# Turning forgetting-attention weights by DMA in 16-bit halves, with the next head's logits ahead of a head's value product

## The chip, the cores and the metric

The kernel runs on one core of a Trainium2 chip. The metric is the device time of one execution, in microseconds (us): the median of several runs. The engines of a core have queues of their own and meet at semaphores: TensorE (PE in the profile, with its weight loads as PEld), VectorE (DVE), ScalarE (ACT), GpSimd (POOL) and SyncE (SP), which here issues nearly all DMA transfers.

## The reference

Two layers act on a sequence of 512 positions of width 1024. Each layer is a SwiGLU half-step, a mixing step, and a second SwiGLU half-step. The change concerns the mixing step, and in it the forgetting attention:

```python
proj = u @ w_in[l]
q_sb, k_sb, v_sb, q_fx, k_fx, v_fx, f_logit, q_mem = split(proj)   # heads: 8 x 64 | 8 x 64 | 4 x 128
o_sb = stick_breaking(q_sb, k_sb, v_sb)
o_fx = forgetting(q_fx, k_fx, v_fx, log_sigmoid(f_logit + b_forget[l]))
o_mem = memory(q_mem, *split(mem_n @ w_mem_kv[l]))
g_sb, g_fx, g_mem = split(sigmoid(u @ w_gate[l] + b_gate[l]))
merged = g_sb * (o_sb @ w_br_sb[l]) + g_fx * (o_fx @ w_br_fox[l]) + g_mem * (o_mem @ w_br_mem[l])
h = h + rmsnorm(merged @ w_out[l])

def forgetting(q, k, v, log_f):           # per head, in four blocks of 128 query positions
    c = cumsum(log_f)
    z = q @ k.T / 8 + c[query] - c[key]
    p = softmax(where(key <= query, z, -inf))
    return p @ v
```

The weights p come out with queries on the partitions. For the value product p @ v the keys have to be on the partitions, so the lower triangle of p, ten blocks of 128 x 128, is transposed.

## The kernel before

**Precision.** Products run in the PE's fp32r format. A value is split into a high part (a cast on ACT) and a low part (a subtraction on DVE) by `split`, lines 182 and 183 of the profile, and a product is the sum of three matmuls (`mm3`, L212 to L214). In the value product of a head, only the weights are split (two matmuls for each of four key blocks).

**What runs beside what.** The mixing step of a layer goes through its heads one after the other: 4 memory heads, 8 stick-breaking heads (tiles with s in their names: `zs`, `ts`, `ns`, `pws`, `pts`, `pvs`), then 8 forgetting heads (tiles with f: `zf`, `pf`, `ptf`, `pvf`). Between a head's steps, PE works on the projections and gates of the same layer (`pq`, `pk`, `pv`, `pg`), of which a list of jobs is kept. A head is a generator that yields either work that it put on PE, `("pe", us)`, or a time that it expects to wait for other engines, `("wait", us)`; `Queue.weave` fills each wait with jobs from the list, as far as a limit for that head allows. Where the list up to the limit is used up, the head goes on at once. The waits are the constants `W_SB0..2` (stick-breaking) and `W_FX0`, `W_FX1` (forgetting). PE's order is so written out; instructions on the other engines which `keep_in_program_order` doesn't hold are put in order by a list scheduler when the program is built. The gates' own evaluation (`ga`: L204 to L208 on ACT and DVE) and the preparation of the branch weights (`wh_wb`, `wl_wb`) also run in this stage. After it come the branch product `pb` (forgetting branch), and the output product (`pwo`).

**A forgetting head** (`fox_head`). Logits go to four banks of PSUM `z`: the causal mask (L1262), q times k (L1269), and the decay (L1270, whose operand `qk` is prepared by `fox_pre` one head ahead). For each query block DVE takes the maximum (L1272), ACT the exponential with its sum (L1274), and DVE the reciprocal and the scaling (L1275, L1276). After a planned wait of 6.5 us `transposed` puts ten transposes on PE (L1185) into the same four banks, and splits the blocks out of PSUM into `ptf`, by four casts on ACT and four subtractions on DVE. After a second wait, of 4.7 us, `attend` multiplies by the values (eight matmuls, L1171, into `pvf`); the sum of the two halves (L1174, L1175) is split into `o`, the operand of the branch product. The heads go in the order of pairs 2, 3, 0, 1, so that the last head of layer 0 is `f0_1_1`. Each head is woven on its own, with a limit of its own.

**A stick-breaking head** turns its weights by another way already. The float32 weights are seen as pairs of 16-bit words. ACT writes the low words and the high words into separate planes (`turn_out`, L1152, tile `ns`), SP issues a DMA transpose of both planes (`turn_over`, L1161, back into `ts`), ACT joins the words again into a float32 tile `pws` (L1237), and the joined tile is split from SBUF in two pieces, 640 and 896 columns wide. This goes by three groups of query blocks: (3,), (2,) and (1, 0), of 1024, 768 and 768 words.

## Time and profile before

| | |
|---|---|
| Time, median of 3 runs | 2339.55 us (2337.33 to 2340.01) |
| Profiled execution: time, span | 2342.67 us, 2340.9 us |
| PE busy | 2322.9 us (99%) |
| DVE busy | 1764.2 us (75%) |
| ACT busy | 1509.8 us (64%) |
| Granted TensorE clock | 0.999 |
| Forgetting heads of layer 0 | about 629 to 766 us of the span |
| Transposes on PE (L1185) | 160, 10 for each of 16 heads |

The profile's rows name the line of the kernel, the engine, the operation and the tiles (out<-in). A timeline row gives the start, the length, and in brackets how long the engine had been idle before and what released it. A row of waits sums the idle time of an engine before a group of instructions by its releaser. Matmuls overlap in the pipeline, so the distance from one start to the next is their cost, not their listed length.

### The profile page before, as it was taken

What the parts mean: (1) busy time and instruction counts of PE and PEld (TensorE: products, weight loads), DVE (VectorE), ACT (ScalarE), POOL (GpSimd) and SP (SyncE); (2) the same over time, 40 slices, a digit from 0 to 9 for tenths busy, and PEclk for the clock granted to TensorE, in tenths of its full rate; (3) what the DMA queues carried; (4) which work ended last, traced back from release to release, by engine and by line L of the source; (5) the groups of instructions that cost most, each with busy time, mean ns of one, the idle gap of its engine ahead of it and who ended that gap; (6) DMA issues with size and microseconds to landing.
All of it is one profiled execution on the core that took longest, in us unless ns stands there. A gap on an engine that the chain in (4) does not pass through costs nothing.

```text
span 2340.9 us, 30650 instructions
## 1 busy us (share of the span) xinstructions
PE 2322.9 (99%) x11463; PEld 1960.2 (84%) x11463; DVE 1764.2 (75%) x2253; ACT 1509.8 (64%) x2216; POOL 81.2 (3%) x182
## 2 busy tenths in 40 slices
PE   9999999999999999999999999999999999999998
PEld 7888888888888888888898888888888888888887
DVE  8877877566777688878798788765677767887785
ACT  6677465577756556775656774655787674667744
POOL 0000000000111000000000000000001100000000
PEclk9999999999999999999999999999999999999999
DMA  6667454344423555674646665544444236466744
GB/s 207 190 176 221 146 189 141 93 115 114 122 73 105 187 186 164 185 199 152 226 144 186 196 185 179 185 114 95 119 105 116 81 118 200 160 195 176 220 138 144
DMA packets 340344, 365.44 MB, mean 156 GB/s; under 512 B 120778, under 2 KB 231650, under 8 KB 340196
## 3 DMA queue, kind: packets, MB, share of 16 engines
q1 hardware_dynamic: 340100, 363.46, 52.0%
q8 instruction: 90, 1.47, 0.3%
q14 instruction: 58, 0.48, 0.1%
q0 software_dynamic: 96, 0.03, 0.0%
HBM read 319.39 MB, written 16.78 MB: 144 GB/s over the span
## 4 chain that ended last, share of the span: by engine, by line
PE 85%; DMA 5%; ACT 4%; DVE 3%; issue 2%; DVEq 0%; SPq 0%; ACTq 0%
PE pg L213 4%; PE pg L212 4%; PE pg L214 4%; PE pda L213 3%; PE pda L212 3%; PE pda L214 3%; PE pdc L213 3%; PE pdc L212 3%; PE pdc L214 3%; PE pb L213 1%; PE pb L212 1%; PE pb L214 1%; PE pq L213 1%; PE pq L212 1%; PE pq L214 1%
## 5 line engine op out<-in xcount | busy, mean ns | idle before, releaser
L212 PE MATMUL pg<-us_a,wh_wg 128*128 128x512 f32 x384 | 150.4, 392 | 0.0
L213 PE MATMUL pg<-us_a,wh_wg 128*128 128x512 f32 x384 | 149.7, 390 | 0.0
L214 PE MATMUL pg<-us_a,wl_wg 128*128 128x512 f32 x384 | 149.6, 390 | 0.0
L183 DVE TENSOR_TENSOR wl_da<-raw_da,wh_da 128x1024 fp32r<-128x1024 f32 x50 | 60.8, 1223 | 44.6 <-ACT wh_da L182 44.4
L183 DVE TENSOR_TENSOR wl_dc<-raw_dc,wh_dc 128x1024 fp32r<-128x1024 f32 x50 | 61.0, 1223 | 44.1 <-ACT wh_dc L182 44.1
L213 PE MATMUL pdc<-wl_dc,ahc 128*128 128x512 f32 x224 | 87.7, 392 | 0.0
L213 PE MATMUL pda<-wl_da,aha 128*128 128x512 f32 x224 | 87.6, 391 | 0.0
L214 PE MATMUL pdc<-wh_dc,alc 128*128 128x512 f32 x224 | 87.2, 389 | 0.0
L214 PE MATMUL pda<-wh_da,ala 128*128 128x512 f32 x224 | 87.2, 389 | 0.0
L212 PE MATMUL pdc<-wh_dc,ahc 128*128 128x512 f32 x224 | 86.6, 390 | 0.5 <-ACT pdc L895 0.5
L212 PE MATMUL pda<-wh_da,aha 128*128 128x512 f32 x224 | 86.5, 389 | 0.0
L186 DVE SCALAR_TENSOR_TENSOR wl_wg<-raw_wg,wh_wg 128x1024 fp32r<-128x1024 f32 x48 | 58.7, 1223 | 35.8 <-ACT wh_wg L185 35.6
L214 PEld LDWEIGHTS pg<-us_a,wl_wg 128*128 128x128 f32 x384 | 72.1, 188 | 15.1
L212 PEld LDWEIGHTS pg<-us_a,wh_wg 128*128 128x128 f32 x384 | 72.1, 188 | 14.2
L213 PEld LDWEIGHTS pg<-us_a,wh_wg 128*128 128x128 f32 x384 | 72.1, 188 | 14.2
L182 ACT CAST wh_da<-raw_da 128x1024 fp32r<-128x1024 f32 x50 | 52.1, 1050 | 46.9 <-PE pda L214 19.4
L182 ACT CAST wh_dc<-raw_dc 128x1024 fp32r<-128x1024 f32 x50 | 52.3, 1049 | 46.0 <-DMA raw_dc<-in_ffn_w_down_dram 13.9
L182 ACT CAST wh_uc<-raw_uc 128x1024 fp32r<-128x1024 f32 x44 | 46.4, 1054 | 34.5 <-PE pwc1g L214 7.7
L182 ACT CAST wh_ua<-raw_ua 128x1024 fp32r<-128x1024 f32 x44 | 46.2, 1052 | 30.2 <-PE pwa0g L214 7.6
L183 DVE TENSOR_TENSOR wl_uc<-raw_uc,wh_uc 128x1024 fp32r<-128x1024 f32 x44 | 53.7, 1220 | 14.5 <-ACT wh_uc L182 14.5
L183 DVE TENSOR_TENSOR wl_gc<-raw_gc,wh_gc 128x1024 fp32r<-128x1024 f32 x40 | 48.5, 1221 | 20.3 <-ACT wh_gc L182 20.3
L1237 ACT COPY pws<-ts 128x1024 uint16<-128x1024 uint16 (+1 forms) x64 | 55.4, 914 | 12.2 <-DMA ts<-ns 11.9
(643 smaller groups left out, 7921.1 us busy)
## 6 DMA issues: line engine op xcount, KB each, us to landing
raw_da<-in_ffn_w_down_dram SPq DMA_DIRECT2D x66, 512.0 KB, 5.3
raw_dc<-in_ffn_w_down_dram SPq DMA_DIRECT2D x66, 512.0 KB, 4.6
raw_ga<-in_ffn_w_gate_dram SPq DMA_DIRECT2D x52, 512.0 KB, 4.7
raw_ua<-in_ffn_w_up_dram SPq DMA_DIRECT2D x52, 512.0 KB, 4.5
raw_gc<-in_ffn_w_gate_dram SPq DMA_DIRECT2D x52, 512.0 KB, 4.1
raw_uc<-in_ffn_w_up_dram SPq DMA_DIRECT2D x52, 512.0 KB, 4.4
raw_wg<-in_w_gate_dram SPq DMA_DIRECT2D x48, 512.0 KB, 3.6
raw_wo<-in_w_out_dram SPq DMA_DIRECT2D x24, 512.0 KB, 3.7
```

The lines of the kernel that those rows point to most:

```text
L182: both = [nc.scalar.copy(h_ap, src)]
L183: make = lambda: nc.vector.tensor_tensor(l_ap, src, h_ap.bitcast(F32), ALU.subtract)
L186: make = lambda: nc.vector.scalar_tensor_tensor(l_ap, src, scale, h_ap.bitcast(F32), ALU.mult, ALU.subtract)
L212: nc.tensor.matmul(pt, lh, rh, start=start, stop=False, skip_group_check=free)
L213: nc.tensor.matmul(pt, lh, rl, start=False, stop=False, skip_group_check=free)
L214: nc.tensor.matmul(pt, ll, rh, start=False, stop=stop, skip_group_check=free)
L1237: nc.scalar.copy(block_words(word, i), over[:, :, c:c + i + 1])
```

## The change

A forgetting head's weights are now turned in the way of a stick-breaking head: three copies on ACT write the word planes (tile `nf`), SP issues three DMA transposes back into `pf`, and the words are joined into `pwf`, here by four copies on DVE, and split in pieces of 640 and 896 columns. The new helper `joined` serves both kinds of head, with the engine of its copies as an argument. The ten transposes, the tile with a triangular layout and the splits from PSUM go. All heads of the stage are now one chain, `foxes`: when a head has reached its last wait (`W_FX2`), the next head is started, and its logits are put on PE before that wait and thus ahead of the first head's value product. The planned waits are 2.0, 6.3 and 5.0 us, and the limit of jobs follows the head that was started last. (In rows of the changed kernel, line numbers after this place are a few lower: `split` is L180 and L181, `mm3` L210 to L212, `attend` L1170, the gates L202 to L206, `turn_out` L1137 and `turn_over` L1146.)

```diff
-                dt = self.step(limit)
+                dt = self.step(limit() if callable(limit) else limit)
...
+    def joined(groups, copy, name):
+
+        word = stile([P, LAST + P], "tri", "pw" + name, F32)
+        nc.gpsimd.memset(word[:, LAST - 2 * P:LAST], 0.0)
+        for rows, w, t in groups:
+            over = t[:, :w].bitcast(U16).rearrange("p (h r q) -> p h r q", h=2, q=P)
+            for i in rows:
+                c = (rows[0] - i) * 2
+                copy(block_words(word, i), over[:, :, c:c + i + 1])
+        tri = stile([P, 2, LAST + P], "tri", "pt" + name)
+        for c in (slice(8 * P, LAST + P), slice(0, 7 * P)):
+            split(tri[:, 0, c], tri[:, 1, c], word[:, c])
+        return tri
+
...
-    def transposed(ptile, name):
-
-        tri = tri_tile("pt" + name)
-        for kt in reversed(range(NT)):
-            pt = pbank("z", f"pt{name}_{kt}")
-            for i in range(kt, NT):
-                tc.keep_in_program_order(
-                    nc.tensor.transpose(pt[:, i * P:(i + 1) * P], ptile[i][:, kt * P:(kt + 1) * P], ident[:]))
-            split(tri_part(tri, 0, kt), tri_part(tri, 1, kt), pt[:, kt * P:].rearrange("p (a b) -> p a b", b=P))
-        return tri
...
     def fox_head(q, k, vts, pj, j, qk, ot, name, ahead):
 
         rc = slice(0, 104 if j == 0 else P)
-        ptile = {}
+        groups = []
         pzs = [pbank("z", f"z{name}_{i}") for i in range(NT)]
         for i, pz in enumerate(pzs):
             nc.tensor.matmul(pz[:, i * P:(i + 1) * P], ident16[:], causal16, start=True, stop=False,
                              skip_group_check=True)
-        for i in reversed(range(NT)):
-            pz = pzs[i]
-            w = (i + 1) * P
-            wp = max(w, 256)
-            qs = slice(i * P, (i + 1) * P)
-            nc.tensor.matmul(pz[:, :wp], q[:, j, qs], k[:, j, :wp], start=False, stop=False, skip_group_check=True)
-            nc.tensor.matmul(pz[:, :wp], qk[rc, 0, qs], qk[rc, 1, :wp], start=False, stop=True, skip_group_check=True)
-            st = sb.tile([P, 2], F32, tag="st", bufs=8, name=f"st{name}_{i}")
-            nc.vector.tensor_reduce(st[:, 0:1], pz[:, :w], AX.X, ALU.max, negate=True)
-            p = tmp(f"p{name}_{i}")
-            nc.scalar.activation(p[:, :w], pz[:, :w], AF.Exp, bias=st[:, 0:1], accum_out=st[:, 1:2])
-            nc.vector.reciprocal(st[:, 1:2], st[:, 1:2])
-            nc.vector.tensor_scalar(p[:, :w], p[:, :w], st[:, 1:2], None, ALU.mult)
-            ptile[i] = p
+        for rows in ((3,), (2,), (1, 0)):
+            w0 = (rows[0] + 1) * P
+            p = tmp(f"p{name}_{rows[0]}")
+            for i in rows:
+                pz = pzs[i]
+                w = (i + 1) * P
+                wp = max(w, 256)
+                qs = slice(i * P, (i + 1) * P)
+                nc.tensor.matmul(pz[:, :wp], q[:, j, qs], k[:, j, :wp], start=False, stop=False, skip_group_check=True)
+                nc.tensor.matmul(pz[:, :wp], qk[rc, 0, qs], qk[rc, 1, :wp], start=False, stop=True, skip_group_check=True)
+                st = sb.tile([P, 2], F32, tag="st", bufs=8, name=f"st{name}_{i}")
+                nc.vector.tensor_reduce(st[:, 0:1], pz[:, :w], AX.X, ALU.max, negate=True)
+                o = p[:, (rows[0] - i) * w0:][:, :w]
+                nc.scalar.activation(o, pz[:, :w], AF.Exp, bias=st[:, 0:1], accum_out=st[:, 1:2])
+                nc.vector.reciprocal(st[:, 1:2], st[:, 1:2])
+                nc.vector.tensor_scalar(o, o, st[:, 1:2], None, ALU.mult)
+            groups.append((rows, w0 + (len(rows) - 1) * P, p))
         yield ("pe", 1.5)
         yield ("wait", W_FX0)
-        tri = transposed(ptile, name)
-        yield ("pe", 1.1)
+        planes = []
+        for rows, w, p in groups:
+            planes.append(tmp(f"n{name}_{rows[0]}"))
+            turn_out(p, w, planes[-1])
+            turn_over(planes[-1], w, p)
+        ahead()
         yield ("wait", W_FX1)
-        ahead()
+        tri = joined(groups, nc.vector.tensor_copy, name)
+        yield ("wait", W_FX2)
         attend(pbank("mm", "pv" + name), j, vts, pj, tri, ot, name)
...
     W_SB0, W_SB1, W_SB2 = 7.0, 7.0, 5.0
-    W_FX0, W_FX1 = 6.5, 4.7
+    W_FX0, W_FX1, W_FX2 = 2.0, 6.3, 5.0
...
-            for at, p in enumerate(FOX):
-                Q.past(marks[1, p], W_K, limits[NP + at][0])
-                for j in range(2):
-                    Q.weave(fox(at, j), limits[NP + at][j])
+            order = [(at, j) for at in range(NP) for j in range(2)]
+            now = [0]
+
+            def foxes():
+
+                def head(n):
+                    at, j = order[n]
+                    Q.past(marks[1, FOX[at]], W_K, limits[NP + at][0])
+                    return fox(at, j)
+                gen = head(0)
+                for n in range(len(order)):
+                    for kind, us_ in gen:
+                        if us_ is W_FX2:
+                            if n + 1 < len(order):
+                                following = head(n + 1)
+                                yield next(following)
+                            now[0] = min(n + 1, len(order) - 1)
+                        yield kind, us_
+                    gen = following
+
+            def limit():
+                at, j = order[now[0]]
+                return limits[NP + at][j]
+            Q.weave(foxes(), limit)
```

What this does to the order of instructions, at the end of the forgetting heads of layer 0 (layer 1 has the same order). The first two are PE's rows from the logits of the last head, `zf0_1_1`, to the branch product `pb`, before and after. `pvf0_1_0` and `pvf0_1_1` are the value products of the last head but one and of the last. Before:

```order
L1171 MATMUL pvf0_1_0_6814<-ptf0_1_0_6739,v0_1_0_0_5692 128x512 x2
...
L1270 MATMUL zf0_1_1_0_6828<-qk0_1_1_6809 128x256
...
L1185 MATMUL ptf0_1_1_3_6911<-ident_65,pf0_1_1_3_6840 128x128
...
L1185 MATMUL ptf0_1_1_0_6926<-ident_65,pf0_1_1_3_6840 128x128
...
L214 MATMUL pg0_1_6_6961<-us_a0_1_2947,wl_wg0_1_3_4_6610 128x512
L1171 MATMUL pvf0_1_1_6977<-ptf0_1_1_6909,v0_1_0_1_5827 128x256 x4
L1171 MATMUL pvf0_1_1_6977<-ptf0_1_1_6909,v0_1_0_0_5692 128x384 x2
L1171 MATMUL pvf0_1_1_6977<-ptf0_1_1_6909,v0_1_0_0_5692 128x512 x2
L212 MATMUL pg0_1_6_6961<-us_a0_1_2947,wh_wg0_1_3_4_6609 128x512
...
L214 MATMUL pg0_1_7_7007<-us_a0_1_2947,wl_wg0_1_3_4_6610 128x512
L212 MATMUL pb0_1_0_7067<-o0_1_0_5577,wh_wb0_1_0_0_6790 128x512
```

After:

```order
L1252 MATMUL zf0_1_1_0_6829<-qk0_1_1_6775 128x256
...
L1170 MATMUL pvf0_1_0_6912<-ptf0_1_0_6824,v0_1_0_1_5807 128x256 x4
L1170 MATMUL pvf0_1_0_6912<-ptf0_1_0_6824,v0_1_0_0_5705 128x384 x2
L1170 MATMUL pvf0_1_0_6912<-ptf0_1_0_6824,v0_1_0_0_5705 128x512 x2
...
L212 MATMUL pg0_1_7_6933<-us_a0_1_2947,wl_wg0_1_3_4_6546 128x512
L1170 MATMUL pvf0_1_1_6985<-ptf0_1_1_6980,v0_1_0_1_5807 128x256
L210 MATMUL pb0_1_0_7027<-o0_1_0_5577,wh_wb0_1_0_0_6721 128x512
L1170 MATMUL pvf0_1_1_6985<-ptf0_1_1_6980,v0_1_0_1_5807 128x256 x3
L1170 MATMUL pvf0_1_1_6985<-ptf0_1_1_6980,v0_1_0_0_5705 128x384
...
L210 MATMUL pb0_1_0_7027<-o0_1_1_5578,wh_wb0_1_0_0_6721 128x512
```

Before, 33 matmuls of the gates or projections stand between a head's logits and its transposes and 24 between these and its value product, at every head but the first, whose numbers are 2 lower; behind the last value product 33 of `pg` are left ahead of `pb`. After, the ten transposes are gone, and there are 42 matmuls from one value product to the next logits and 24 from logits to the value product of the head before. So from a head's logits to its own value product there stand 24 + 42 + 24 matmuls and two small steps of its neighbours at the middle heads, 42 + 24 and one such step at the first, and 24 + 24 and one such step at the last; behind the last value product no `pg` is left.

The same place on ACT, after: the rows from the value product of the last head but one to the word planes of the last head (`nf0_1_1`). Before, the last head had four casts of `ptf0_1_1` here, of 128 to 512 columns.

```order
L1173 COPY sf0_1_0_6921<-pvf0_1_0_6912 64x512
L206 ACTIVATE ga0_1_5_6868<-ga0_1_5_6868,bgate_79 128x512
L202 ACTIVATE ga0_1_6_6926<-pg0_1_6_6887,nbgate_78 128x512
L180 CAST o0_1_1_5578<-sf0_1_0_6921 64x512
L203 ACTIVATE ga0_1_6_6926<-ga0_1_6_6926 128x512
L180 CAST wh_wb0_1_2_0_6875<-raw_wb0_1_2_0_6725 128x1024
L204 ACTIVATE ga0_1_6_6926<-ga0_1_6_6926,one_t_73 128x512
L1137 COPY nf0_1_1_3_6946<-pf0_1_1_3_6837 128x1024
L180 CAST wh_wb0_1_3_0_6881<-raw_wb0_1_3_0_6731 128x1024
L206 ACTIVATE ga0_1_6_6926<-ga0_1_6_6926,bgate_79 128x512
L1137 COPY nf0_1_1_2_6949<-pf0_1_1_2_6845 128x768
L1137 COPY nf0_1_1_1_6952<-pf0_1_1_1_6853 128x768
```

The three copies of the last head's words stand behind the sum, the gates and two weight casts, that is, behind nine other instructions from the value product of the head before.

And on SP, after: the last head's three transposes among the loads of the output weights (`raw_wo`) and a store of gates (`gsave`). Before, SP had no transposes here.

```order
L254 DMA raw_wo0_0_0_6879<-in_w_out_dram 128x2x512
L1146 DMA_TRANSPOSE pf0_1_1_3_6837<-nf0_1_1_3_6946 128x8x128
L254 DMA raw_wo0_0_2_6885<-in_w_out_dram 128x2x512
L1458 DMA gsave0<-ga0_1_6_6926 128x512
L1146 DMA_TRANSPOSE pf0_1_1_2_6845<-nf0_1_1_2_6949 128x6x128
L1146 DMA_TRANSPOSE pf0_1_1_1_6853<-nf0_1_1_1_6952 128x6x128
```

The second and third transposes stand behind a load, and behind a store that waits for the end of gate 6.

More of the change, by code (lines that the diff above doesn't have):

```diff
@@ L77 @@
     NC = 2
-    TRI = (0, 512, 896, 1152)
-    TRIW = 1280
     QLO = (0, 128, 256, 256)
@@ L1170, in attend @@
                 tc.keep_in_program_order(
-                    nc.tensor.matmul(pv[:, lo:], v, tri_part(tri, part, kt, kt * P - lo), start=(kt == NT - 1 and part == 0),
+                    nc.tensor.matmul(pv[:, lo:], v, square_part(tri, part, kt, kt * P - lo), start=(kt == NT - 1 and part == 0),
                                      stop=(kt == 0 and part == 1), skip_group_check=True))
```

24 lines of the change are left out of this document (3 added, 21 removed).

## The prediction

> **What bounds the kernel now.** I read the page's head, then PE's waits, then the forgetting heads of layer 0 in four windows.
>
> ```profile
> span 2340.9 us, 30650 instructions
> PE 2322.9 (99%) x11463; PEld 1960.2 (84%) x11463; DVE 1764.2 (75%) x2253; ACT 1509.8 (64%) x2216; POOL 81.2 (3%) x182
> ```
>
> PE is busy 99% of the span. All its idle time is 2340.9 - 2322.9 = 18.0 us. So PE sets the time, and a matmul less is time less, provided that nothing makes PE wait instead. Its waits:
>
> ```profile
> PE pwo L213 <- DVE wl_wo L183: 2.6, 4, 0.9
> PE pvs L1171 <- DVE pts L183: 1.4, 2, 0.7
> ...
> PE pga L668 <- ACT w_ga L182: 0.2, 1, 0.2
> ```
>
> (Line, releaser, total us, times, longest.) The list ends here; no wait of a forgetting head (`zf`, `ptf`, `pvf`) is in it. A stick-breaking head's value product (`pvs`) does wait for its weights, twice, and that is the way the forgetting heads now take. The windows (us, then busy time of PE, PEld, DVE, ACT, POOL, then the granted clock, the DMA share and GB/s):
>
> ```profile
> 629.00:660.00 31.00, 31.00 (x207) 28.08 (x206) 23.52 (x50) 18.68 (x39) 3.78 (x8) 1.00 0.29 86
> 660.00:690.00 30.00, 30.00 (x155) 25.21 (x154) 22.30 (x46) 19.73 (x40) 5.59 (x10) 1.00 0.19 54
> 690.00:720.00 30.00, 30.00 (x157) 25.29 (x156) 22.77 (x49) 18.79 (x40) 5.60 (x10) 1.00 0.22 70
> 720.00:760.00 40.00, 40.00 (x208) 33.67 (x207) 29.77 (x61) 27.92 (x56) 2.51 (x5) 1.00 0.42 139
> ```
>
> PE is busy all the time in this stage. Here time comes from PE's work alone, and there is no wait for the change to remove. DVE is at 98.4 of 131 us, 75%; DMA and SP have room.
>
> **The gain: 160 transposes.** All of them, and the last head's surroundings on PE:
>
> ```profile
> L1185 PE MATMUL ptf<-ident,pf x160: 270/272/273, 638.5 to 1918.9; 128*128 128x128 f32 x160
> L182 ACT CAST ptf<-ptf x64: 242/430/617, 639.7 to 1919.5; 128x128 fp32r<-128x128 f32 x16, 128x256 fp32r<-128x256 f32 x16, 128x384 fp32r<-128x384 f32 x16, 128x512 fp32r<-128x512 f32 x16
> L183 DVE TENSOR_TENSOR ptf<-ptf,ptf x64: 279/484/692, 641.0 to 1920.4; 128x128 fp32r<-128x128 f32 x16, 128x256 fp32r<-128x256 f32 x16, 128x384 fp32r<-128x384 f32 x16, 128x512 fp32r<-128x512 f32 x16
> ```
>
> ```profile
> 757.40 1.25 PE L1185 MATMUL ptf<-ident,pf 128*128 128x128 f32 x10
> 758.41 0.47 PE L212 MATMUL pg<-us_a,wh_wg 128*128 128x512 f32 x1
> 758.72 0.40 PE L213 MATMUL pg<-us_a,wh_wg 128*128 128x512 f32 x1
> ...
> 763.75 0.39 PE L214 MATMUL pg<-us_a,wl_wg 128*128 128x512 f32 x1
> 763.97 1.45 PE L1171 MATMUL pvf<-ptf,v 128*128 128x256 f32 x8
> 765.26 0.40 PE L212 MATMUL pg<-us_a,wh_wg 128*128 128x512 f32 x1
> ```
>
> The listed 272 ns overlap. Ten transposes take 758.41 - 757.40 = 1.01 us, and the matmul behind them takes 0.31 us to the next start where others take 0.23: 1.09 us a head, 8.7 us a layer, 17.4 us in all. Further numbers from these rows: 24 gate matmuls take 763.97 - 758.41 = 5.56 us (0.23 each), a value product 765.26 - 763.97 = 1.29 us.
>
> **What comes onto the other engines.** DVE loses four subtractions from PSUM (medians near 0.28, 0.42, 0.55, 0.69 us by the row above: 1.9 us) and gains two from SBUF of 640 and 896 columns and four copies of 16-bit words, 2560 elements a row in all. No copy of this kind runs on DVE before. Nearest rows:
>
> ```profile
> L183 DVE TENSOR_TENSOR pts<-pws,pts 128x640 fp32r<-128x640 f32 x16 | 13.2, 824 | 16.3 <-ACT pts L182 16.3
> L183 DVE TENSOR_TENSOR pts<-pws,pts 128x896 fp32r<-128x896 f32 x16 | 17.4, 1090 | 3.1 <-ACT pts L182 3.1
> L1276 DVE TENSOR_SCALAR pf<-pf,stf 128x512 f32<-128x512 f32 x8 | 3.8, 474 | 0.0
> L1276 DVE TENSOR_SCALAR pf<-pf,stf 128x128 f32<-128x128 f32 x8 | 2.4, 304 | 0.2
> ```
>
> The subtractions cost 0.82 + 1.09 = 1.9 us, as much as those removed. A one-operand operation from SBUF costs 0.44 ns an element and 0.25 us besides (474 and 304 ns); a subtraction 1.08 ns and 0.14 us (279 and 692 ns). So the four copies cost 2560 x 0.44 ns + 4 x 0.25 = 2.1 us at the one rate and 2560 x 1.08 ns + 4 x 0.14 = 3.3 us at the other. I take 2.1, since a copy has one operand and both sides in SBUF, like L1276, and keep 3.3 as a rival. The head period is 66 matmuls and two small steps (24 + 42 at 0.23, and 2 x 1.3): 17.8 us; DVE has 0.75 x (17.8 + 1.1) = 14.2 us of work in it before, 16.3 us after, 92%. It fits, with little room.
>
> *A page on it:* the Trainium skill, "VectorE: DVE Perf Modes", section "What auto-detection actually checks", gives two elements a cycle for one source with source and destination in SBUF, and reserves four for 16-bit tensors with step 1; the joined words have step 2 in their destination, so by it the lower of my two prices holds. No row of before shows such a copy.
>
> ACT loses four casts of `ptf` (0.24 to 0.62, 1.7 us) and gains three word copies and two casts; by the windows it is busy 60 to 70%, and on average it has room. SP gains 48 transposes:
>
> ```profile
> L1161 SPq DMA_TRANSPOSE ts<-ns x48: 1209/1232/2306, 441.9 to 1776.6; - x48
> DMA to landing us min/median/max: 2.7/3.2/5.8
> ```
>
> That is 1.23 us of SP and 3.2 us to landing for each. PE's waits name no transfer in this stage, and 3 x 1.23 us of a period of 17.8 is free on SP: nothing, by itself. The memsets and the copies of `qk` on POOL stay off the path: 0, POOL is under 20% busy. If one of these covers is gone, PE waits at a value product.
>
> **What happens at each head.** A value product needs: logits, maxima, exponentials, scaling, word copies (ACT), transposes (SP), joins (DVE), casts (ACT), subtractions (DVE). How long that takes, the stick-breaking heads show, whose chain is of the same kind:
>
> ```profile
> 585.09 1.45 PE L1210 MATMUL zs<-k,q 128*128 128x512 f32 x8
> 590.84 1.05 ACT L1152 COPY ns<-ts 128x1024 uint16<-128x1024 uint16 x1
> 592.75 0.81 ACT L1152 COPY ns<-ts 128x768 uint16<-128x768 uint16 x1
> 594.19 0.83 ACT L1152 COPY ns<-ts 128x768 uint16<-128x768 uint16 x1 [0.62 <-DVE ts L1223]
> 601.48 0.94 ACT L182 CAST pts<-pws 128x896 fp32r<-128x896 f32 x1
> 602.46 1.09 DVE L183 TENSOR_TENSOR pts<-pws,pts 128x896 fp32r<-128x896 f32 x1 [0.76 <-ACT pts L182]
> ```
>
> From the end of the logits (586.5) to the last subtraction (603.55): 17.0 us. PE's order gives the cover, from the logits to the second half of the value product (its first four matmuls and a `pb` matmul are some 0.9 us):
>
> - Middle heads, 1 to 6: 24 + 42 + 24 matmuls and two steps, 20.5 + 2.6 = 23.1 us. Enough by 6 us against 17.0. Their word copies, too, may stand behind other work on ACT, so I take 0 and keep up to 1 us each for the rival with a full DVE.
> - First head: 42 + 24 and one step, 16.4 us, and 0.9. Against 17.0: 0 to 1.5, I take 0.3 a layer.
> - Last head: 24 + 24 and one step: 5.56 + 1.29 + 5.56 = 12.4 us, and 0.9: 13.3. The list of jobs is used up there; the 33 `pg` matmuls that stood behind its value product are consumed earlier. By the stick-breaking head alone PE waits 17.0 - 13.3 = 3.7 us.
>
> For the last head ACT's order makes it later. Before, ACT's rows after a value product were:
>
> ```profile
> 764.41 0.72 ACT L208 ACTIVATE ga<-ga,bgate 128x512 f32<-128x512 f32 x1 [0.82 <-DVE ga L207]
> 765.46 0.58 ACT L1174 COPY sf<-pvf 64x512 f32<-64x512 f32 x1 [0.32 <-PE pvf L1171]
> 766.80 0.62 ACT L182 CAST o<-sf 64x512 fp32r<-64x512 f32 x1 [0.76 <-DVE sf L1175]
> 767.53 0.69 ACT L204 ACTIVATE ga<-pg,nbgate 128x512 f32<-128x512 f32 x1
> 768.25 0.63 ACT L205 ACTIVATE ga<-ga 128x512 f32<-128x512 f32 x1
> 768.92 0.72 ACT L206 ACTIVATE ga<-ga,one_t 128x512 f32<-128x512 f32 x1
> 770.02 1.06 ACT L182 CAST wh_wb<-raw_wb 128x1024 fp32r<-128x1024 f32 x1 [0.38 <-PE pg L213]
> ```
>
> After, the last head's three word copies stand behind such rows, and the first of these waits for the value product of head 6, which ends 5.56 + 1.29 = 6.85 us after the logits. The walk from there, in us after the logits: ACT does 0.58 + 0.72 + 0.69 + 0.62 + 0.63 + 1.06 + 0.72, the first word copy 1.05, then 1.06 + 0.72, then 0.81 + 0.83: 9.5 us, so the last copy ends at 16.4 (15.4 if rows overlap by 0.1 us each, as the last two above do). SP issues the second transpose from about 15.6, the third from 16.8; it lands 3.2 us later, at 20.0. Two joins at 0.44 ns (0.8 us), the cast 0.94, the subtraction 1.09 and hand-overs: 23.0. With the earlier copies 21.9. I take 22.5: PE waits 22.5 - 13.3 = **9.2 us** a layer, between 3.7 and 11.7 (ACT 2 us late). Behind it the branch product has about ten matmuls (2.3 us) on the first pair before it needs the sum of the last head, whose copy, addition and cast take about as long: 0.
>
> **The clock after such a wait.** Nothing in the stage shows PE after an idle time of several us. The nearest row is from the start of the kernel:
>
> ```profile
> 8.46 2.03 PE L1661 MATMUL utx<-ident,fx 128*128 128x128 f32 x8
> ```
>
> There eight transposes take 2.03 us, 0.25 each, where the ten at 757.40 take 1.25, 0.125 each: half the rate, and that up to 10.3 us of the span at least. A wait of 9 us may cost as little as nothing or as much as the kernel's start, 10.3 us at half rate, a loss of 5.2. The wait is cut in two by the first half of the value product and is not a cold start, so I take about half of that: 2.5 us a layer.
>
> *A page on it:* the Trainium skill, "TensorE: Matmul & The Clock Gate", section "What's actually happening", says that the array's clock halves after an idle window of about 3.4 us and comes back after about 3.4 us of sustained work. By it each long wait loses some 1.7 us, or up to 3.4 with the window's phase, and the sum below moves by -1.6 to +1.8 us. The kernel's start agrees with a slow phase (0.25 against 0.125 us); no row of before shows one after a wait.
>
> **The sum.** Per layer: -8.7 (transposes) + 9.2 (last head) + 0.3 (first head) + 2.5 (slow rate) = +3.3. Twice: +6.6 us on the profiled execution's 2342.67, that is 2349.3. That execution stood 3.1 us above the median of the three runs and 1.8 us above its own span; on the median the sum is 2339.55 + 6.6 = **2346**.
>
> **Rivals.** A difference of 0.2%, 4.7 us, or 2.35 a layer, is about what a measurement can tell from no change.
>
> - *The last head's chain is as short as a stick-breaking head's* (faster). For it: ACT is only about 65% busy, and the scheduler's order need not be the order in which things come free. Against it: ACT runs its queue in order. The wait is then 3.7 us, with 1.0 for the slow rate: -8.7 + 3.7 + 0.3 + 1.0 = -3.7 a layer, 2332. It decides where the second half is ready: with 1.0 for the rate before 13.3 + 5.1 = 18.4 us after the logits the kernel is faster; with 2.5 behind 13.3 + 8.3 = 21.6 it is slower.
> - *No wait at all*: 2339.55 - 17.4 = 2322. Only if the weights were ready 13.3 us after the logits; no chain of this kind shows that.
> - *DVE becomes the bound*: the copies run at 1.08 ns an element, 3.3 us a head. DVE then needs 17.5 of 17.8 us, the middle heads wait 1 us each and the last 0.8 more: +6.8 a layer, 2346 + 13.6 = 2360. For it: the strided 16-bit destination. Against it: L1276's rate.
> - *The slow rate lasts as long as at the kernel's start*: 5.2 instead of 2.5 a layer, 2346 + 5.4 = 2351. For it: the wait of 9 us comes near to a start. Against it: no row shows any loss after a wait.
>
> **Chances.** My forecast 0.56, of which 0.24 falls within 0.2% of no change, since a wait 1 us shorter or a small loss of rate does that, and 0.32 above; short chain 0.14; no wait 0.04; DVE full 0.14; long slow rate 0.12. Faster: 0.14 + 0.04 = 0.18. Same: 0.24. Slower: 0.32 + 0.14 + 0.12 = 0.58. The range takes in the short chain and the long slow rate and nearly all of a full DVE: 2331 to 2358; the forecast's own is 2340 to 2351.
>
> **What would show it.** PE's waits get a new row, `pvf` released by DVE `ptf`, two large waits of about 4 and 5 us a layer near the end of each layer's forgetting heads, and none of the size at the middle heads. The stage's other rows are shorter by 1.1 us a head. The matmuls behind the wait have 0.4 us from start to start instead of 0.23, for some us. The DVE copies show about 0.36 us (256) and 0.7 us (1024). If PE stays without a gap in this stage, the walk on ACT was wrong, and the time is near 2322. If waits appear at every head, it is DVE.

## The result and the profile after

The changed kernel takes 2362.28 us (median of 5 runs, 2357.57 to 2364.14) against 2339.55 us: ratio 1.0096, 95% interval 1.0082 to 1.0111. It is slower by 22.7 us, where I had forecast 6.6, and 4 us beyond the range.

The page's head, and PE's waits (line, releaser, total us, times, longest):

```profile
span 2355.8 us, 30462 instructions
PE 2310.8 (98%) x11303; PEld 1947.8 (83%) x11303; DVE 1795.6 (76%) x2285; ACT 1546.7 (66%) x2232; POOL 88.8 (4%) x182
```

```profile
PE pvf L1170 <- ACT ptf L180: 23.3, 2, 11.8
PE pb L210 <- DVE ga L205: 3.9, 2, 2.0
PE pvf L1170 <- DVE ptf L181: 1.9, 4, 0.6
PE pg L210 <- DVE k L181: 1.3, 2, 0.6
```

PE is 12 us less busy: 17 us of transposes are gone, and other matmuls take longer. It has waits that it did not have, these four kinds. The largest is one of 11.6 to 11.8 us in each layer, before a value product, for the cast of the weights. The forgetting heads of layer 0 in windows (us, busy PE, PEld, DVE, ACT, POOL, granted clock, DMA share, GB/s):

```profile
660.00:690.00 30.00, 30.00 (x142) 24.91 (x141) 26.46 (x51) 22.67 (x42) 6.23 (x10) 1.00 0.42 98
690.00:720.00 30.00, 29.37 (x142) 24.00 (x141) 24.02 (x41) 20.33 (x33) 6.64 (x9) 1.00 0.44 113
720.00:760.00 40.00, 37.51 (x171) 30.46 (x170) 34.82 (x69) 33.22 (x61) 3.85 (x7) 0.96 0.49 132
760.00:780.00 20.00, 8.45 (x38) 6.64 (x37) 9.60 (x16) 14.75 (x21) 0.00 (x0) 0.81 0.82 220
```

The big hole is at 760 to 780, where the DMA share rises from 0.49 to 0.82 and the granted clock falls to 0.81. PE there:

```profile
759.91 0.39 PE L212 MATMUL pg<-us_a,wl_wg 128*128 128x512 f32 x1
760.14 1.45 PE L1170 MATMUL pvf<-ptf,v 128*128 128x256 f32 x8
...
778.61 0.58 PE L1170 MATMUL pvf<-ptf,v 128*128 128x256 f32 x1 [11.55 <-ACT ptf L180]
```

At 760.14 is the value product of the last head but one; 24 gate matmuls follow it, and then PE waits 11.55 us for the last head.

From the first logits of the forgetting heads to the first matmul of the output product, PE's time adds up as follows (us; each kind's distances from start to start, waits taken out):

| | before, layer 0 / 1 | after, layer 0 / 1 |
|---|---|---|
| whole stage | 164.8 / 164.8 | 175.6 / 177.1 |
| transposes on PE | 8.1 / 8.1 | none |
| waits of PE | 0 / 0 | 14.7 / 15.9 |
| value products `pvf` | 10.4 / 10.4 | 12.4 / 12.7 |
| branch products `pb` | 43.7 / 43.7 | 45.9 / 46.0 |
| everything else | 102.7 / 102.7 | 102.6 / 102.5 |

The stages got 10.8 + 12.2 = 23.0 us longer together, as much as the medians differ by. The two spans differ by 14.9 us only, since the profiled execution of the changed kernel is the shortest of its five (2357.57 us) and that of before stood above its median. What made the rest of that execution 8 us shorter I can't say; the change has no instruction there, and some 3 us of it are waits of PE (10.6 us outside the two stages before, 7.5 after). In the fifteen profiles of this document the rest takes 2002 to 2011 us, so a few us between two single executions say little about an edit; the stages say more.

### The profile page after: what moved, and what is told of

It is laid out like the page before. It is cut to its first block, busy times and chain, and to the rows that moved or that the text cites. A ratio compares the mean times of both kernels' runs of the same rounds, so it can differ in the third digit from the quotient of the medians.

```text
span 2355.8 us, 30462 instructions
## 1 busy us (share of the span) xinstructions
PE 2310.8 (98%) x11303; PEld 1947.8 (83%) x11303; DVE 1795.6 (76%) x2285; ACT 1546.7 (66%) x2232; POOL 88.8 (4%) x182
## 4 chain that ended last, share of the span: by engine, by line
PE 82%; DVE 6%; DMA 5%; ACT 5%; issue 2%; DVEq 0%; SPq 0%; ACTq 0%
PE pda L211 3%; PE pda L210 3%; PE pda L212 3%; PE pg L210 2%; PE pg L211 2%; PE pg L212 2%; PE pdc L211 2%; PE pdc L212 2%; PE pdc L210 2%; DMA pf<-nf 2%; PE pb L210 2%; PE pb L211 2%; PE pb L212 1%; PE pwc0g L210 1%; PE pwc1g L211 1%
## 5 line engine op out<-in xcount | busy, mean ns | idle before, releaser
L210 PE MATMUL pg<-us_a,wh_wg 128*128 128x512 f32 x384 | 150.1, 391 | 1.3 <-DVE k L181 1.3
L212 PE MATMUL pg<-us_a,wl_wg 128*128 128x512 f32 x384 | 149.5, 389 | 0.0
L181 DVE TENSOR_TENSOR wl_da<-raw_da,wh_da 128x1024 fp32r<-128x1024 f32 x50 | 60.8, 1223 | 45.9 <-ACT wh_da L180 45.9
L181 DVE TENSOR_TENSOR wl_dc<-raw_dc,wh_dc 128x1024 fp32r<-128x1024 f32 x50 | 61.0, 1223 | 43.4 <-ACT wh_dc L180 43.4
L212 PE MATMUL pda<-wh_da,ala 128*128 128x512 f32 x224 | 87.2, 389 | 0.0
L212 PE MATMUL pdc<-wh_dc,alc 128*128 128x512 f32 x224 | 87.2, 389 | 0.0
L210 PE MATMUL pdc<-wh_dc,ahc 128*128 128x512 f32 x224 | 86.5, 389 | 0.0
L210 PE MATMUL pda<-wh_da,aha 128*128 128x512 f32 x224 | 86.5, 389 | 0.0
L210 PEld LDWEIGHTS pg<-us_a,wh_wg 128*128 128x128 f32 x384 | 72.4, 188 | 16.7 <-PE pb L212 2.0
L212 PEld LDWEIGHTS pg<-us_a,wl_wg 128*128 128x128 f32 x384 | 72.1, 188 | 15.3
L180 ACT CAST wh_dc<-raw_dc 128x1024 fp32r<-128x1024 f32 x50 | 52.3, 1050 | 47.5 <-DMA raw_dc<-in_ffn_w_down_dram 16.1
L180 ACT CAST wh_da<-raw_da 128x1024 fp32r<-128x1024 f32 x50 | 52.1, 1049 | 46.8 <-PE pda L212 14.1
L180 ACT CAST wh_uc<-raw_uc 128x1024 fp32r<-128x1024 f32 x44 | 46.4, 1054 | 38.0 <-PE pwc1g L212 9.2
L180 ACT CAST wh_ua<-raw_ua 128x1024 fp32r<-128x1024 f32 x44 | 46.2, 1053 | 32.9 <-PE pwa1g L212 9.3
L181 DVE TENSOR_TENSOR wl_uc<-raw_uc,wh_uc 128x1024 fp32r<-128x1024 f32 x44 | 53.7, 1220 | 16.7 <-ACT wh_uc L180 16.7
L183 ACT ACTIVATE wh_wg<-raw_wg 128x1024 fp32r<-128x1024 f32 x48 | 50.6, 1058 | 19.3 <-PE pv L1123 7.7
L181 DVE TENSOR_TENSOR wl_ga<-raw_ga,wh_ga 128x1024 fp32r<-128x1024 f32 x40 | 48.4, 1219 | 18.7 <-ACT wh_ga L180 18.7
```

What stands on the lines that cost most here:

```text
L180: both = [nc.scalar.copy(h_ap, src)]
L181: make = lambda: nc.vector.tensor_tensor(l_ap, src, h_ap.bitcast(F32), ALU.subtract)
L183: both = [nc.scalar.activation(h_ap, src, AF.Copy, scale=scale)]
L210: nc.tensor.matmul(pt, lh, rh, start=start, stop=False, skip_group_check=free)
L212: nc.tensor.matmul(pt, ll, rh, start=False, stop=stop, skip_group_check=free)
```

## The experiments

Four theories stood at first. *1:* the last head lacks cover: the matmuls that could stand between its logits and its value product are used up. *2:* VectorE is too full, at every head. *3:* ScalarE is as near to its limit. *4:* the last head is late because of ScalarE's order. Others came up on the way. All times are medians beside runs of the kernel before (2338.86 to 2339.55 us), with the ratio to it and its interval.

**1. Fewer matmuls between the heads, so that some are left for the last.**

```diff
-    W_FX0, W_FX1, W_FX2 = 2.0, 6.3, 5.0
+    W_FX0, W_FX1, W_FX2 = 2.0, 4.3, 5.0
```

> Planned wait W_FX1 4.3 instead of 6.3 us: from one value product to the next logits 33 matmuls instead of 42, so that 57 matmuls and not 24 are left between the value products of the last two heads, 81 and one step (19.7 us) from the last head's logits to its value product, and 30 behind it. All else as in the changed kernel. Theory 1 (the last head lacks cover: PE waits 11.6 us there, since the jobs are used up): most of the wait goes, 0 to 4 us is left a layer; the middle heads have 21.2 instead of 23.1 us of cover and wait 0 to 3 us more. Time 2340 to 2348. Theory 2 (the loss is that VectorE is too full at every head): less matmul work a head makes VectorE's share higher, the waits at the middle heads grow by 2 us a head, and the time stays at 2358 or above.

Measured: 2337.27 us, ratio 0.9989 (0.9980 to 0.9998), faster than theory 1 forecast. The waits of 11.6 us are gone, with one constant changed. The waits left are small and many:

```profile
PE pvf L1170 <- DVE ptf L181: 7.6, 9, 1.0
PE pvf L1170 <- ACT ptf L180: 1.9, 3, 1.1
```

Theory 1 holds for the bulk of the loss, against theory 2.

**2. The last head of each layer keeps its transposes on PE.**

```diff
...
         yield ("pe", 1.5)
+        if name.endswith("1_1"):
+            yield ("wait", 1.0)
+            ahead()
+            tri = transposed(groups, name)
+            yield ("pe", 1.1)
+            yield ("wait", 4.7)
+            attend(pbank("mm", "pv" + name), j, vts, pj, tri, ot, name)
+            yield ("pe", 1.2)
+            return
         yield ("wait", W_FX0)
```

> The last head of each layer keeps the old way: 6 matmuls behind the value product before it its ten transposes on PE, then 18 matmuls, then its value product. The other seven heads as in the changed kernel. Theory 1 (cover of the last head): the wait of 11.6 us and the slow matmuls behind it (about 1.5 us) go, ten transposes (1.1 us) and a wait for the splits of about 1.3 us come: 10 to 11 us a layer less, time 2340 to 2342, with the small waits of the middle heads (3 us a layer and 2 us of slow clock) unchanged. Theory 2 (VectorE everywhere): less than 5 us in all, 2357 or above.

Measured: 2341.22 us, 1.0011 (1.0001 to 1.0020), as theory 1 had it. The last head alone is worth 21 us against the changed kernel. The wait of `pb` for `ga` stayed, 2.0 us a layer.

**3. The joining copies on ScalarE.**

```diff
-        tri = joined(groups, nc.vector.tensor_copy, name)
+        tri = joined(groups, nc.scalar.copy, name)
```

> The joining copies of the forgetting heads on ScalarE (3.8 us a head by the stick-breaking heads' rows) instead of VectorE (2.1 us). Theory 2 (VectorE is late at the middle heads): their waits, 2.6 to 3.7 us a layer and 2 us of slow clock behind them, go; the last head's wait grows by about 1.7 us; time 2354 to 2358. Theory 3 (ScalarE, in order, is as near to its limit): waits at the middle heads grow instead, time 2366 or above.

Measured: 2365.99 us, 1.0114 (1.0099 to 1.0129), at the rival's side. Relieving VectorE of 2.2 us a head doesn't remove the waits of the middle heads; a wait of 2.2 us of `pb`, now released by VectorE's sum, stands in the same place, and the last head's wait is 12.2 and 12.5 us.

**4. The last head's word copies right behind its logits.**

```diff
                                 yield next(following)
+                                if n + 2 == len(order):
+                                    next(following)
+                                    next(following)
```

> The last head's three word copies and transposes are written right behind its logits, so that on ScalarE they stand directly behind its exponentials and ahead of the gates, the weight casts and the sum of the head before; PE's order is unchanged. Theory 4 (the last head is late because of ScalarE's order and the transfers that its transposes then meet): the last word copy ends 9 to 10 us after the logits instead of 16.1, the second half of the weights is ready after 17 to 18 us instead of 26, the wait falls from 11.6 to 4 or 5 us; time 2346 to 2350. Rival (the chain is bound elsewhere, by VectorE or by the transfers' own time): the wait stays above 8 us, time above 2355.

Measured: 2346.09 us, 1.0028 (1.0017 to 1.0040). ScalarE now does the three copies at once, directly behind the exponentials, and ends them at 762.1 us of the span; in the changed kernel it is 770.8:

```profile
759.61 2.50 ACT L1137 COPY nf<-pf 128x1024 uint16<-128x1024 uint16 x3
```

The waits at the last value product fell to 2.6 us in layer 0 and 3.8 in layer 1. PE's order up to that product and its cover are the same as in the changed kernel, so 16 of the 23 us hang on where three copies and their transposes stand. The edit moves both: the copies stand ahead of the gates on ScalarE, and the transposes, issued from 760.67 us on, are ahead of the loads of output weights. Experiment 12 takes the loads away alone. Theories 1 and 4 are two sides of one thing: a chain too long for its cover.

**5. PE kept busy through the wait.**

```diff
...
         yield ("wait", W_FX2)
+        if name.endswith("1_1"):
+            for _ in range(52):
+                tc.keep_in_program_order(nc.tensor.matmul(pzs[0][:], ident16[:], fillw[:], start=True, stop=True))
         attend(pbank("mm", "pv" + name), j, vts, pj, tri, ot, name)
```

> As the changed kernel, with 52 matmuls of zeros (bf16, 128x512, into a logits bank that is no longer read) on PE ahead of the last head's value product, so that PE is busy through most of the 11.6 us for which it waited. They compute nothing that is used. Theory 5 (the slow matmuls behind the wait come from PE's having been idle): value product and branch product behind the wait go at full rate, the granted clock stays at 1.0, 1.5 us a layer less: 2358 to 2361. Rival (they are slow because their operands come late): no change in their spacing, 2361 to 2364.

Measured: 2356.68 us, 1.0072 (1.0058 to 1.0086), below both forecasts. The granted clock at 772 to 780 us is 1.00, against 0.51 in the changed kernel. PE's rows (line numbers are two higher here; the row of the fill shows 50 of its 52 matmuls):

```profile
727.18 0.50 PE L212 MATMUL pb<-o,wh_wb 128*128 128x512 f32 x1 [1.96 <-DVE ga L207]
...
766.45 11.18 PE L1275 MATMUL zf<-fillw,ident 128*128 128x512 bf16 x50
780.13 0.38 PE L1172 MATMUL pvf<-ptf,v 128*128 128x256 f32 x1 [2.50 <-ACT ptf L182]
...
783.52 0.63 PE L212 MATMUL pb<-o,wh_wb 128*128 128x512 f32 x1
```

PE still waits 2.5 us behind the fill (1.9 in layer 1), and the half rate comes behind this shorter wait. From the last head's value product on, value and branch products take 25.1 and 25.3 us in the two layers, where the changed kernel takes 25.1 and 24.9 and the kernel before 23.1. So the clock follows PE's idle time, as theory 5 has it, but the run saved none of the slow matmuls and gives no price for them. What is shorter, by 1.9 and 2.2 us a layer, are value and branch products ahead of the fill: in this execution no slow matmuls follow the wait for a PSUM bank (the last section shows why). The two stages together are 0.6 us shorter than in the changed kernel, and the profiled executions differ by 0.7; the 5.6 us between the medians stay unexplained.

**6 and 7. 36 or 39 matmuls, and all the rest ahead of the last value product.** With W_FX1 4.9 and 5.6 us:

```diff
...
-        yield ("wait", W_FX2)
+        yield ("wait", 15.0 if name.endswith("1_1") else W_FX2)
```

> W_FX1 4.9 us, so that 36 matmuls stand from a value product to the next logits (42 in the changed kernel, 33 in the first experiment), and the last head waits for all the rest, 66 matmuls, ahead of its value product: cover of 84 matmuls and two steps (21.9 us) at the middle heads, 90 and one step (21.7 us) at the last. Theory 1: the small waits of the first experiment at the value products (0.5 to 1.1 us each, 5.5 us a layer) shrink by about 0.7 us each, the last one goes; 2331 to 2336. Rival (the waits for a PSUM bank held by a late gate, 2 us and as much again of slow clock a layer, come back as the logits shift): 2338 to 2342.

> W_FX1 5.6 us: 39 matmuls, cover of 22.6 us at the middle heads, and 24 + 45 matmuls and one step (17.0 us) at the last, which needs 21 or more: there PE waits about 4 us. Middle heads nearly free of waits at the value products. Theory 1: 2336 to 2341, above the kernel with 36. Rival (the last head is not what limits): 2330 to 2334, below it.

Measured: 2348.52 us, 1.0047 (1.0034 to 1.0061), with 36; 2337.89 us, 0.9994 (0.9986 to 1.0003), with 39. The second came as theory 1 had it (2.6 and 1.1 us of waits at the last head in layer 0). The first missed both forecasts. It is slower than 33 and than 39, with waits of 1.6 and 1.7 us at two middle heads, most of its waits being released by VectorE's subtraction:

```profile
PE pvf L1170 <- DVE ptf L181: 13.5, 17, 1.7
```

Its stages have 15.9 us of waits in all, those with 33 have 10.3 and those with 39 have 11.0; and the granted clock is 0.5 for 13.7 us of them, against 3.4 and 6.8. A few matmuls more or less shift the logits against the gates, and the order on VectorE and ScalarE changes with it. Which of its rows makes 36 worse I have not found.

**8. The DMA transposes alone,** each head woven on its own, logits behind the value product as before the change.

```diff
...
-            Q.weave(foxes(), limit)
+            for at, p in enumerate(FOX):
+                Q.past(marks[1, p], W_K, limits[NP + at][0])
+                for j in range(2):
+                    Q.weave(fox(at, j), limits[NP + at][j])
```

> The DMA transposes alone: each head is woven on its own as before the change, its logits behind the value product of the head before, with the three planned waits: 66 matmuls (15.0 us) from a head's logits to its value product, 24 (5.5 us) at the last. With a chain of 17 to 22 us from logits to weights PE waits 2 to 7 us at each of seven heads and 12 to 17 at the last, 8.7 us of transposes are saved: 20 to 55 us a layer more than before, 2380 to 2450. Rival (the order is worth little): waits as in the changed kernel, below 2370.

Measured: one run, 2356.24 us, far below the forecast of 2380 to 2450 and where the rival had it. The last head waits 10.6 us in each layer, the others at most 1.6 us at a cover of 15.0 us:

```profile
PE pvf L1170 <- ACT ptf L180: 23.3, 5, 10.6
PE pvf L1170 <- DVE ptf L181: 7.4, 10, 1.6
```

So a middle head's chain is at most some 16.6 us long when no other head's logits stand in it. With the logits ahead the cover is 23.4 us and there are waits all the same: the added cover was eaten by a longer chain. The last head shows it best. Its first weights are ready 16.2 us after its logits here (cover 5.6, wait 10.6) and 23.9 us after them in the changed kernel (cover 12.4, wait 11.55): moving the logits ahead gained nothing there.

**9. The residual's loads out of the way of the last transposes.**

```diff
-                nc.sync.dma_start(hT[i][:], hsave[i])
+                tc.keep_in_program_order(nc.sync.dma_start(hT[i][:], hsave[i]))
```

> As the changed kernel, but the four loads that bring the residual back (hm, 512 KB each) are queued on SP behind what was written before them, so that none of them runs beside the last head's transposes. Theory 6 (those transposes land after 4.7 to 6.2 us instead of 2.8 to 3.2 because the DMA engines are full there): they land after 3 to 4.5 us, the wait of 11.6 us gets 1.5 to 2.5 us shorter, time 2357 to 2360. Rival (they are slow for another reason, such as their order among themselves): landing times and wait as in the changed kernel, 2361 to 2364.

Measured: 2361.72 us, 1.0096 (1.0083 to 1.0110): no difference. The second and third transposes land after 5.4 and 4.8 us, and the wait is 12.5 us. That these loads delay them is refuted.

**10. Experiments 7 and 4 together.**

> 39 matmuls from a value product to the next logits, all the rest (45) ahead of the last head's value product, as in the seventh experiment, and the last head's word copies written right behind its logits, as in the fourth. By theories 1 and 4 the last head's waits of 3.7 us a layer and the slow matmuls behind them (about 2 us) go: 2328 to 2333. Rival (they move to the branch product, which then waits for the last head's sum or for a bank): 2335 to 2339.

Measured: 2340.62 us, 1.0004 (0.9996 to 1.0013). The forecast of 2328 to 2333 failed, and the rival's of 2335 to 2339 too. In the profile the last head still waits (2.9 us in layer 0, 1.6 in layer 1), with its word copies early; its stages, 164.3 and 164.5 us, are a little shorter than those of experiment 7 (166.4 and 165.4), the median is not. Whether it is any better than experiment 7 stays open.

**11. Experiment 2 with 39 matmuls,** and 21 and 24 around the last head's transposes (W_FX1 5.6 us; waits of 3.9 and 6.5 us at the last head).

> The second experiment (last head by the old way) with 39 matmuls instead of 42 at the other heads, and 21 and 24 around the last head's transposes. The wait for the bank (2 us a layer) and the slow clock behind it (2 us) go, the last head has no wait: -17.4 + 2.2 for its transposes + 2 to 4 us a layer of small waits: 2329 to 2333. Rival (the waits for a bank stay or move): 2336 to 2341.

Measured: 2334.04 us, 0.9977 (0.9966 to 0.9987): faster than both kernels, by 4.9 us against before, if less than forecast. No wait of these stages is over 0.9 us, the one for the bank is gone:

```profile
PE pvf L1186 <- DVE ptf L181: 3.8, 6, 0.9
```

**12. The loads of the output weights, too, behind the last transposes.** With the edit of experiment 9; `turned` is the last transpose, and the loads are written once the last head is through.

```diff
...
+            if self.name.startswith("wo") and Q.turned is not None:
+                tc.add_manual_dep(ins.ins, Q.turned.ins.name, mybir.DependencyInfo(
+                    mybir.DependencyClass.NoSync, mybir.DependencyReason.DATA), reason="behind")
...
```

> The ninth experiment (the residual's loads behind the last head's transposes) and also the loads of the output weights (raw_wo, 512 KB each), of which one stood on SP directly ahead of the first and one ahead of the second of those transposes: all are now queued behind the third. Theory 7 (a DMA transpose is slow when a 512 KB load was issued up to about 1 us ahead of it: in the runs so far 309 such took 5.3 us in the median, 518 without a load in the 3.5 us before them 3.0): the last head's transposes land after 2.8 to 3.5 us, the wait falls from 11.6 to 8.5 to 9.5 us, time 2355 to 2358, unless the output product then waits for its weights. Rival (they are slow for another reason at this place): 4.7 us or more as before, 2361 to 2364.

Measured: 2356.05 us, 1.0072 (1.0057 to 1.0087). SP's rows of the changed kernel at this place, and the median landing time of its three transposes (at the end of the row of DMA issues):

```profile
767.46 0.38 SPq L254 DMA_DIRECT2D raw_wo<-in_w_out_dram  x1
767.94 1.23 SPq L1146 DMA_TRANSPOSE pf<-nf  x1
769.97 0.39 SPq L254 DMA_DIRECT2D raw_wo<-in_w_out_dram  x1
770.40 0.47 SPq L1458 DMA_DIRECT2D gsave<-ga  x1
770.91 3.16 SPq L1146 DMA_TRANSPOSE pf<-nf  x2
```

```profile
pf<-nf SPq DMA_TRANSPOSE x3, 5.1
```

and of this experiment:

```profile
768.22 1.23 SPq L1153 DMA_TRANSPOSE pf<-nf  x1
769.79 0.34 SPq L1465 DMA_DIRECT2D gsave<-ga  x1
770.51 2.55 SPq L1153 DMA_TRANSPOSE pf<-nf  x2
773.18 1.31 SPq L254 DMA_DIRECT2D raw_wo<-in_w_out_dram  x2
```

```profile
pf<-nf SPq DMA_TRANSPOSE x3, 2.8
```

Without a 512 KB load ahead of them the transposes land after 2.8 us, and the wait is 7.2 us in layer 0 and 9.2 in layer 1 instead of 11.6 and 11.8. The theory holds. Experiment 4 left 2.6 and 3.8 us; so of what it removed, 4.4 and 2.6 us can be the loads, and the larger part, 4.6 and 5.4 us, is ScalarE's order.

**13. The order alone,** with ten transposes on PE as before the change.

```diff
-    W_FX0, W_FX1, W_FX2 = 2.0, 6.3, 5.0
+    W_FX0, W_FX1, W_FX2 = 6.5, 4.7, 0.01
...
+        yield ("wait", W_FX0)
+        tri = transposed(groups, name)
+        yield ("pe", 1.1)
+        yield ("wait", W_FX1)
+        ahead()
```

> The order alone: ten transposes on PE and planned waits of 6.5 and 4.7 us as before the change, and the next head's logits ahead of a head's value product. Theory 1 (the order costs nothing by itself, the lack of cover at the last head does): no long wait, time within 4 us of the kernel before, 2336 to 2343. Rival (the exponentials of the next head, which now stand on ScalarE ahead of the gates and the sum of the head before, hold a PSUM bank and make PE wait 2 us or more a layer): 2344 to 2350.

Measured: 2338.15 us, 0.9995 (0.9985 to 1.0004). PE has no wait at all in either stage. The swapped order costs nothing where the spacing is as before; but the next head's logits stand only 3 matmuls ahead of a value product here, and not 24 as in the change.

## Why the prediction was wrong

The direction, the main place and its mechanism came true: PE is the bound, the transposes left (8.1 us a layer, and 0.2 on the matmuls behind them; 8.7 forecast), the jobs run out at the last head, and ScalarE's order makes that head late. The sum was 12.0 us of losses a layer; 19.1 and 20.6 were measured (stage plus transposes saved). Three terms were too small: the last head's wait by 2.4 and 2.6 us, the middle heads' by 3.1 and 4.1, the slow matmuls by 1.8 and 2.2; the first head's 0.3 did not come (0 and 0.1). By its steps:

- *"What comes onto the other engines"*: right. The four copies:

```profile
L1156 DVE COPY pwf<-pf 128x1024 uint16<-128x1024 uint16 x16 | 12.1, 756 | 13.5 <-DMA pf<-nf 13.4
L1156 DVE COPY pwf<-pf 128x256 uint16<-128x256 uint16 x16 | 4.9, 306 | 0.1
```

With those of 768 and 512 (0.64 and 0.54 us) 2.2 us a head, where I took 2.1. From 256 to 1024 an element costs 0.59 ns, nearer the 0.44 that I took than the 1.08 of a subtraction. The Trainium skill ("VectorE: DVE Perf Modes", "What auto-detection actually checks") gives two elements a cycle for such a copy; the trace agrees in so far as 0.59 is about half of 1.08.

- *Last head, the walk on ScalarE*: right. Its copies were to end 16.4 us after the logits, and end at 770.76, which is 16.1 us behind 754.68:

```profile
769.21 1.55 ACT L1137 COPY nf<-pf 128x768 uint16<-128x768 uint16 x2
...
777.83 1.65 ACT L180 CAST ptf<-pwf 128x640 fp32r<-128x640 f32 x2 [3.02 <-DVE pwf L1156]
```

- *"it lands 3.2 us later"*: this term failed. The third transpose was issued at 18.0 us (16.8 forecast), and the last two landed after 6.2 and 5.1 us, because of the two loads of output weights ahead of them (experiment 12). The second so landed at 777.1 and the third at 777.8: both halves of the weights came at once, and instead of the two waits of about 4 and 5 us that were to show it PE has one. The median of the stick-breaking heads was the wrong price, although its row had a maximum of 5.8: I had seen in the order of SP that a load stands ahead of the second transpose, and took it for a question of SP's time alone. The wait was 11.6 us instead of 9.2, the edge of what I had allowed.

- *"Middle heads, 1 to 6 … I take 0"*: this step failed. They lose 3.1 us of waits in layer 0 and 4.1 in layer 1, of which 2.0 in each layer in one place, where PE waits for a PSUM bank:

```profile
721.59 0.69 ACT L1256 ACTIVATE pf<-zf,stf 128x512 f32<-128x512 f32 x1 [0.42 <-DVE stf L1254]
...
723.27 0.69 ACT L202 ACTIVATE ga<-pg,nbgate 128x512 f32<-128x512 f32 x1
...
724.19 0.63 ACT L203 ACTIVATE ga<-ga 128x512 f32<-128x512 f32 x1
724.86 0.72 ACT L204 ACTIVATE ga<-ga,one_t 128x512 f32<-128x512 f32 x1
...
725.81 0.74 DVE L205 SCALAR_TENSOR_TENSOR ga<-pg,bgate,ga 128x512 f32<-128x512 f32 x1
```

```profile
724.26 0.39 PE L212 MATMUL pg<-us_a,wl_wg 128*128 128x512 f32 x1
726.61 0.50 PE L210 MATMUL pb<-o,wh_wb 128*128 128x512 f32 x1 [1.97 <-DVE ga L205]
```

The gate's evaluation stands on ScalarE among the next head's exponentials, and its bank comes free only behind the last row that reads it (`pg`), on VectorE. I had weighed the head's own chain against its cover, and not what the moved logits push back on ScalarE: the waits of others. This wait of 1.9 to 2.0 us stands in both layers of all six profiles with 42 matmuls and the joins on VectorE; with another spacing (experiments 1, 6, 7, 10, 11 and 13) it doesn't appear there. That ScalarE's order is its cause is read from these rows, and no run has changed that order alone.

- *"The clock after such a wait"*: the size was nearly right, and the term incomplete. 2.5 us a layer was taken. Behind the long wait, value and branch products take 2.0 and 1.9 us more than before; the slow rate lasts 3.9 us there. But value and branch products together got 4.3 and 4.7 us longer. Another 1.6 and 1.8 us stand in the earlier branch products, nearly all of it as slow matmuls behind the wait for the bank, which I had not seen coming. What is left, 0.7 and 1.0 us, sits in the value products of the other heads, whose weight loads wait without a gap on PE.

- *Rivals.* "DVE becomes the bound" gave 2360, near the time, and is not the mechanism: the copies cost what I took, and moving them away did not make the kernel faster (experiment 3). "As short as a stick-breaking head's" is what experiment 4 makes of the last head, by an order of ScalarE that the change does not have. The slow rate did not last as long as at the kernel's start: 3.9 us against 10.3.

## What to carry to other kernels

Where a pipeline hides a longer chain behind work from a list, count what the list has left at the last turn: here the last head had 48 matmuls of cover where the middle ones had 90, which cost 12 us a layer, and one smaller constant gave them back. A step moved ahead brings its followers on the other in-order engines with it; look at what then stands behind them, and by the rows of the middle heads above all at whatever holds a PSUM bank. No order that was tried got the whole gain: with the long waits away, 4.9 us at most of the 15 to 17 us saved on PE reached the time.

## What the runs showed of the hardware

- **A DMA transpose behind a large load is slow.** In the thirteen profiles from before to experiment 11, 672 transposes with no 512 KB transfer issued in the 3.5 us ahead of them landed after 3.0 us in the median; 336 with such a transfer up to 1.2 us ahead after 5.5 us (3.4 to 8.1); 418 with one between 1.2 and 3.5 us ahead after 3.5 us. (The expectation of experiment 12 has an earlier count over fewer profiles.) Experiment 12 shows the cause for one place.

- **A wait of 2 us can halve PE's rate, somewhat later.** Behind the wait for the bank in the changed kernel, PE goes on for 1.3 us, mostly at full rate, and then takes 0.43 us from start to start for 3.0 us:

```profile
727.18 0.39 PE L212 MATMUL pb<-o,wl_wb 128*128 128x512 f32 x1
...
728.32 0.63 PE L210 MATMUL pb<-o,wh_wb 128*128 128x512 f32 x1
728.75 0.63 PE L211 MATMUL pb<-o,wh_wb 128*128 128x512 f32 x1
...
731.28 0.39 PE L211 MATMUL pg<-us_a,wh_wg 128*128 128x512 f32 x1
```

In experiment 11 two waits of 0.64 and 0.78 us within 2 us did the same; in experiment 5 the wait of 1.96 us did not. The traces' record of the granted clock shows what decides it. In each of the fifteen runs the record changes only at the edges of intervals of 3.41 us that follow each other without a break. Of the twelve waits for this bank (the changed kernel and experiments 2, 4, 5, 9 and 12), six lie wholly in one interval, with 1.96 to 1.98 us idle, and in the next the clock is 0.5. The other six are cut by an edge, with at most 1.86 us in one interval, and none is followed by a lower clock. It holds outside these waits too: away from the program's start and end, all 24 intervals at full clock in which PE was idle for 1.96 us or more are followed by 0.5, of those with 1.28 to 1.88 us 8 of 34, of those with less none. So whether a wait of 2 us costs another 1.6 us depends on where in an interval it falls. The Trainium skill ("TensorE: Matmul & The Clock Gate", "What's actually happening") has the clock fall after an idle window of about 3.4 us. The length of the interval agrees with that figure; the idle time in it was shorter.
